# Attention scores from stacked key halves in two fp32r passes, and the third block attended whole ahead of the last slab's second half

## The chip, the cores and the metric

The kernel runs on one core of a Trainium2 chip. The metric is the time of one execution in microseconds of device time; the times below are medians over runs on the chip. A profiled execution gives the trace that the views are taken from: its own time is a little larger than its span, which goes from the first to the last recorded instruction.

## The reference

A trunk of two layers over 512 tokens of width 1024, all in float32. Each layer has a mixer and a PEER stage (16384 experts, product-key routing). The part that the change touches is the first of the mixer's three branches, differential attention with 4 heads, two 64-wide maps per head and blocks of 128 queries:

```python
def block(args):
    qi, bi = args
    s = jnp.einsum('bqhmd,bkhmd->bhmqk', qi, k).astype(jnp.float32) * scale
    qpos = bi * Q_BLOCK + jnp.arange(Q_BLOCK)
    mask = kpos[None, :] <= qpos[:, None]
    p = jax.nn.softmax(jnp.where(mask, s, -jnp.inf), axis=-1)
    a = p[:, :, 0] - lam * p[:, :, 1]
    return jnp.einsum('bhqk,bkhe->bqhe', a.astype(v.dtype), v)
```

The other two branches are a gated short convolution over 256 channels and gated linear attention (GLA). The three outputs are concatenated and multiplied by `w_out`, and the result is added to the residual `x`.

## The kernel before

**How products are made.** Nearly all large products run in float32r, a form of float32 that TensorE takes in one pass with fewer bits. Each operand is kept as a high half (the value rounded to float32r) and a low half (what the rounding left). `split` (L83) makes them: ScalarE copies the value into the high half, VectorE subtracts that from the value into the low half. `mm3` (L77) then adds three products: high by high (L79), high by low (L80), low by high (L81). The small products (scores, transposes, the product with the values) run in plain float32: one such matmul of the program shows as two TensorE instructions in the trace, each with its own weight load.

**The mixer** (L221). The input projection is done in column slabs of 256: `across` (L268) gives channels on the partitions and 512 tokens along the row, `down` (L277) gives tokens on the partitions. Each slab loads its weights in four pieces, splits them, and runs 48 or 96 matmuls. The order is: gate and value slabs, GLA's queries and keys, attention's queries and keys (tiles `qT` and `kT`, 128 partitions = 2 maps x 64 dims, 4 heads, 512 tokens), rotary turning of both (`rope`, L463, which writes its results back by DMAs from GpSimd's queue, L471), attention's values (tile `va`), and the convolution's three slabs 2048, 1792 and 1536 (L378, L381, L393). GLA's steps are strewn between the slabs (`fill`).

**Attention.** There are four query blocks of 128. Block `tb` sees (tb+1)*128 keys, so its score products are 128, 256, 384 and 512 wide. For each block `turned_queries` (L473) copies the two maps of the queries into a tile `qz` whose other 64 partitions are zero (cleared once per layer at L369), so that a contraction over all 128 partitions of `kT` counts one map alone. `head_weights` (L479) makes for one head and each of its two maps, called a score half below, one plain float32 product (L486) and one bfloat16 product with the causal mask (L487) into the same PSUM tile; then come the maximum, the exponentials and the difference of the two maps (L488 to L498). `diff_attention` (L502) transposes the weights (L512) and multiplies them by the values (L516). Blocks 0 and 1 are attended around the convolution's slabs (L375, L380), two heads of block 2 between the two halves of the last slab (L395), the rest of block 2 and block 3 inside the output projection's loop (L434).

**The output projection.** When the slabs' pools close, a pool `wout` opens (L400) with `woraw`, `mh`, `ml`, `woh` and `wol`. Its eight pieces of weights are loaded and split; `out_proj` (L420) takes the token blocks in turn, its last operands being the attention outputs `mh` and `ml`.

**The next stage.** `peer` (L709) opens a pool `ustream` whose tiles are `uraw` (3 x 4 KB per partition), `uwa` (2 x 8 KB), `uwb` (2 x 8 KB) and `ht`, in the order of first use. It loads and splits the first three pieces of the query weights (L778 to L783; the splits show as L729 and L730), and runs their products over the first 256 tokens (L787) while the last token block of the mixer is being normed.

**What sets the order.** The framework schedules the instructions at compile time: an instruction goes where its inputs are ready on the engine, and among those that are ready the order of the program decides. On the chip each engine then works off its list in that order. Memory is handed out as a stack: a pool that opens after another was closed gets the same addresses, and its tiles wait, each for itself, for the last use of what lay there. On the left side the mixer's pool `mix` comes first (`dgain`, `cw`, `qT`, `kT`, `va` and small ones), then the slabs' pools; `wout` opens where the slabs' pools began, and `ustream` where `mix` began.

## Time and profile before

| | |
|---|---|
| median of 3 runs | 2962.35 us (2961.81 to 2962.88) |
| the profiled execution: time | 2958.37 us |
| the profiled execution: span | 2956.6 us |
| TensorE busy | 2925.6 us, 99% of the span |
| VectorE busy | 2394.7 us, 81% |
| ScalarE busy | 1256.3 us, 42% |
| GpSimd busy | 716.0 us, 24% |
| mean granted TensorE clock | 0.999 |

The two mixers lie at about 0 to 269 us and, with its first products made at the end of the first PEER stage, from about 1480 to 1737 us. A line of the timeline gives start, duration, engine, source line, operation, output and inputs, shapes and a count of merged instructions; what stands in brackets is idle time of the engine ahead of it and what ended it. TensorE's matmuls are pipelined, so the duration of one is longer than the step from its start to the next start; it is the step that counts for the time. "PEld" is the weight load, which can run beneath the matmul ahead of it.

### The profile page before, as it was taken

The page shows a single profiled execution, that of the slowest core. Times are in us where ns is not written, and L with a number is a line of the kernel's source. Part 1 is how long each engine was busy: PE and PEld are TensorE (multiplying, and loading weights), DVE is VectorE, ACT ScalarE, POOL GpSimd, SP SyncE. Part 2 cuts the span into 40 slices and gives each one's busy share as a digit, 9 for nine tenths or more (in the row PEclk, how much of TensorE's full clock was granted, in tenths as well). Part 3 has the DMA queues.
Part 4 walks back from the last instruction along what each step waited for, and adds up shares of the span by engine and source line. Part 5 has one row for each costly group of instructions (what it writes and reads, how often), then busy time and mean ns, then how long its engine had stood idle before and what let it go on. Part 6 is the DMA issues. An engine that isn't in the chain of part 4 may idle for free.

```text
span 2956.6 us, 44538 instructions
## 1 busy us (share of the span) xinstructions
PE 2925.6 (99%) x16262; PEld 2606.0 (88%) x16262; DVE 2394.7 (81%) x4754; ACT 1256.3 (42%) x1860; POOL 716.0 (24%) x617
## 2 busy tenths in 40 slices
PE   8999999999999999999999999999999999999998
PEld 7878899999999999888888788999999999988887
DVE  6676999976887788877866769999768787888778
ACT  6253355665333332333453433556653333333333
POOL 1200000222444455222012000012225444452220
PEclk9999999999999999999999999999999999999999
DMA  4322257999999998999633222679999999989995
GB/s 130 92 72 77 93 172 250 321 301 362 348 338 326 330 346 310 368 333 342 251 96 90 67 82 86 205 253 330 303 351 356 333 337 332 332 316 358 346 347 203
DMA packets 335835, 760.24 MB, mean 257 GB/s; under 512 B 30688, under 2 KB 191360, under 8 KB 331520
## 3 DMA queue, kind: packets, MB, share of 16 engines
q1 hardware_dynamic: 160624, 435.19, 41.4%
q0 software_dynamic: 75776, 271.62, 26.0%
q10 hardware_dynamic: 99216, 50.60, 5.7%
q8 instruction: 127, 2.08, 0.3%
q14 instruction: 92, 0.75, 0.1%
HBM read 673.15 MB, written 81.00 MB: 255 GB/s over the span
## 4 chain that ended last, share of the span: by engine, by line
PE 84%; DVE 11%; ACT 2%; issue 2%; DMA 1%; SPq 0%; DVEq 0%; ACTq 0%
PE pv L80 11%; PE pv L81 11%; PE pv L79 11%; PE psh L79 9%; PE psh L81 9%; PE psh L80 9%; PE psp L80 2%; PE psp L81 2%; PE psp L79 2%; PE psq L80 2%; PE psq L79 2%; PE psq L81 2%; PE pss L486 1%; PE psg L1211 1%; PE pss L764 1%
## 5 line engine op out<-in xcount | busy, mean ns | idle before, releaser
L827 POOL DMA_INDIRECT row<-in_u_rows,idx x256 | 349.1, 1363 | 1337.6 <-DVE row L834 627.8
L80 PE MATMUL pv<-vl,wh 128*128 128x512 f32 x1500 | 583.9, 389 | 0.4 <-DVE vl L931 0.3
L81 PE MATMUL pv<-vh,wl 128*128 128x512 f32 x1500 | 583.4, 389 | 0.0
L79 PE MATMUL pv<-vh,wh 128*128 128x512 f32 x1500 | 583.2, 389 | 0.0
L827 POOL DMA_INDIRECT row<-in_v_rows,idx x256 | 315.7, 1233 | 597.0 <-DVE yacc L843 548.2
L745 ACT ACTIVATE ht<-psh 128x384 f32<-128x384 f32 x256 | 125.7, 491 | 742.1 <-PE psh L81 741.9
L931 DVE TENSOR_TENSOR vl<-vraw,vh 128x1024 fp32r<-128x1024 f32 x250 | 305.9, 1224 | 115.2 <-ACT vh L936 104.2
L79 PE MATMUL psh<-ahi,uwb 128*128 128x384 f32 x1024 | 346.9, 339 | 0.0
L79 PE MATMUL psh<-ahi,uwa 128*128 128x384 f32 x1024 | 346.4, 338 | 0.0
L81 PE MATMUL psh<-ahi,uwa 128*128 128x384 f32 x1024 | 344.6, 337 | 0.7 <-DVE uwa L730 0.7
L80 PE MATMUL psh<-alo,uwa 128*128 128x384 f32 x1024 | 344.3, 336 | 0.0
L80 PE MATMUL psh<-alo,uwb 128*128 128x384 f32 x1024 | 344.2, 336 | 0.0
L81 PE MATMUL psh<-ahi,uwb 128*128 128x384 f32 x1024 | 344.1, 336 | 0.0
L81 PEld LDWEIGHTS pv<-vh,wl 128*128 128x128 f32 x1500 | 281.4, 188 | 59.6 <-DVE wl L931 1.0
L80 PEld LDWEIGHTS pv<-vl,wh 128*128 128x128 f32 x1500 | 281.4, 188 | 56.6 <-DVE vl L931 2.2
L79 PEld LDWEIGHTS pv<-vh,wh 128*128 128x128 f32 x1500 | 281.6, 188 | 53.9
L843 DVE SCALAR_TENSOR_TENSOR yacc<-row,wk,yacc 128x1024 f32<-128x1024 f32 x254 | 325.2, 1280 | 1.7
L944 ACT CAST wh<-ht 128x384 fp32r<-128x384 f32 x250 | 127.9, 512 | 433.6 <-DVE ht L1096 417.0
L834 DVE SCALAR_TENSOR_TENSOR row<-row,xg 128x1024 f32<-128x1024 f32 x256 | 308.0, 1219 | 0.0
L730 DVE TENSOR_TENSOR uwa<-uraw,uwa 128x1024 fp32r<-128x1024 f32 x144 | 175.7, 1223 | 134.7 <-ACT uwa L729 134.5
L936 ACT CAST vh<-vraw 128x1024 fp32r<-128x1024 f32 x250 | 262.6, 1050 | 9.7 <-DMA vraw<-in_v_rows 9.7
L730 DVE TENSOR_TENSOR uwb<-uraw,uwb 128x1024 fp32r<-128x1024 f32 x144 | 175.8, 1222 | 105.9 <-ACT uwb L729 105.9
(361 smaller groups left out, 5708.6 us busy)
## 6 DMA issues: line engine op xcount, KB each, us to landing
uraw<-in_peer_u SPq DMA_DIRECT2D x256, 512.0 KB, 5.6
vraw<-in_v_rows SPq DMA_DIRECT2D x256, 512.0 KB, 6.5
G<-stg ACTq DMA_DIRECT2D x48, 1024.0 KB, 7.6
g<-G SPq DMA_DIRECT2D x32, 1536.0 KB, 10.0
H<-ht SPq DMA_DIRECT2D x144, 192.0 KB, 4.7
ht<-H SPq DMA_DIRECT2D x144, 192.0 KB, 6.5
wraw<-in_w_in SPq DMA_DIRECT2D x84, 256.0 KB, 3.2
uraw<-in_peer_w_q SPq DMA_DIRECT2D x32, 512.0 KB, 3.5
```

What stands on the lines that cost most here:

```text
L79: mm(ps, ah, bh, start=first, stop=False)
L80: mm(ps, ah, bl, start=False, stop=False)
L81: mm(ps, al, bh, start=False, stop=last)
L486: nc.tensor.matmul(ps[:, 0:nk], qz[:, h, m], kT[:, h, 0:nk], start=True, stop=False)
L730: self.last = pin(nc.vector.tensor_tensor(lo, src, hi.bitcast(F32), op=OP.subtract))
L745: pin(nc.scalar.activation(hs[c], ps, AF.Gelu))
L827: nc.gpsimd.indirect_dma_start(out=r, out_offset=None, in_=ins[name], in_offset=bass.IndirectOffsetOnAxis(ap=idx[:, k:k + 1], axis=0))
L834: nc.vector.scalar_tensor_tensor(r, r, 1.0, xg, op0=OP.mult, op1=OP.mult, accum_out=hd[:, k:k + 1])
L843: nc.vector.scalar_tensor_tensor(yacc, r, wk[:, k:k + 1], yacc, op0=OP.mult, op1=OP.add)
L931: self.last = pin(nc.vector.tensor_tensor(lo, src, hi.bitcast(F32), op=OP.subtract))
L936: pin(nc.scalar.copy(vh[c], vs[c]))
L944: pin(nc.scalar.copy(wh[c], hs[c]))
```

## The change

The queries and keys are split into high and low halves as float32r. For each map m the tile `ks[m]` holds, on the 64 partitions of that map, the high halves of its keys, and on the other 64 partitions the low halves of the same keys, brought there by a DMA from GpSimd's queue. `qa` holds the high halves of the queries on both halves of the partitions (again by a DMA), `qb` the low halves. One pass over 128 partitions gives high by high plus high by low; a second pass over the 64 partitions of the map gives low by high. `qz`, its clearing and `turned_queries` go.

The order changes with it: the first two blocks' keys and queries are split and stacked ahead of slab 2048, block 0 is attended behind that slab, then the other keys and block 2's queries are stacked, block 1 is attended behind slab 1792, and the whole of block 2 between the two halves of slab 1536. Block 3 stays in the output projection's loop. `qT` and `kT` move out of `mix` into a pool `rawqk` of their own, which opens behind `mix` and closes with the slabs' pools.

```diff
             cw = mp.tile([P, 2, 3], F32, name="cw")
-            qT = mp.tile([P, 4, T], F32, name="qT")
-            kT = mp.tile([P, 4, T], F32, name="kT")
             va = mp.tile([P, TB, T], F32, name="va")
+            wc = mc.enter_context(ExitStack())
+            raw_qk = wc.enter_context(tc.tile_pool(name="rawqk", bufs=1, reuse_waits="tile"))
+            qT = raw_qk.tile([P, 4, T], F32, name="qT")
+            kT = raw_qk.tile([P, 4, T], F32, name="kT")
...
-            with ExitStack() as wc:
+            with wc:
...
-                qz = [ap.tile([P, 4, 2, P], F32, name=f"qz{i}", bufs=1) for i in range(2)]
-                for t in qz:
-                    nc.gpsimd.memset(t, 0.0)
+                ks = [ap.tile([P, 4, T], F32R, name=f"ks{i}", bufs=1) for i in range(2)]
+                kl = wc.enter_context(tc.tile_pool(name="klow", bufs=2, side="right", reuse_waits="tile"))
+                half = [slice(64 * m, 64 * m + 64) for m in range(2)]
+
+                def stack_keys(tb):
+                    t = slice(tb * P, tb * P + P)
+                    lo = kl.tile([P, 4, P], F32R, tag="klo", name="klo")
+                    for m in range(2):
+                        r = half[m]
+                        self.split(ks[m][r, :, t], lo[r], kT[r, :, t])
+                        nc.gpsimd.dma_start(ks[m][half[1 - m], :, t], lo[r])
+
+                def stack_queries(tb):
+                    qa = ap.tile([P, 2, 4, P], F32R, tag="qa", name="qa")
+                    qb = ap.tile([P, 4, P], F32R, tag="qb", name="qb")
+                    for m in range(2):
+                        r = half[m]
+                        self.split(qa[r, m], qb[r], qT[r, :, tb * P:tb * P + P])
+                        nc.gpsimd.dma_start(qa[half[1 - m], m], qa[r, m])
+                    return qa, qb
...
-                attend(0)
+                stack_keys(0)
+                qs[0] = stack_queries(0)
+                stack_keys(1)
+                qs[1] = stack_queries(1)
                 z = qp.tile([P, 2, T + 2], F32, tag="z", name="z", bufs=1)
                 nc.vector.memset(z[:, :, 0:2], 0.0)
                 for j, ps in across(2048):
                     nc.scalar.copy(z[:, j, 2:], ps)
-                attend(1)
+                attend(0)
+                for tb in (2, 3):
+                    stack_keys(tb)
+                qs[2] = stack_queries(2)
                 for j, ps in across(1792):
                     nc.vector.tensor_tensor(z[:, j, 2:], ps, z[:, j, 2:], op=OP.mult)
+                attend(1)
+                qs[3] = stack_queries(3)
...
                 for j, ps in across(1536):
                     if j == 0:
-                        self.turned_queries(2, qT, qz[0])
-                        early = [self.head_weights(2, h, kT, qz[0], lam, ap) for h in range(2)]
+                        attend(2)
                     nc.vector.tensor_tensor(ys[j], ys[j], ps, op=OP.mult)
...
                 for tb in range(TB):
-                    if tb > 1:
-                        attend(tb, early if tb == 2 else ())
+                    if tb > 2:
+                        attend(tb)
...
         for m in range(2):
             ps = self.psA.tile([P, T], F32, tag="a", name="pss")
-            nc.tensor.matmul(ps[:, 0:nk], qz[:, h, m], kT[:, h, 0:nk], start=True, stop=False)
+            r = slice(64 * m, 64 * m + 64)
+            nc.tensor.matmul(ps[:, 0:nk], qs[0][:, m, h], ks[m][:, h, 0:nk], start=True, stop=False)
+            nc.tensor.matmul(ps[:, 0:nk], qs[1][r, h], ks[m][r, h, 0:nk], start=False, stop=False)
             nc.tensor.matmul(ps[:, tb * P:nk], self.identb, self.causal, start=False, stop=True)
```

19 lines of the change are left out of this document (6 added, 13 removed).

## The prediction

> **What bounds the kernel now.** I read the page first: the busy shares, then the chain that ended last.
>
> ```profile
> PE 2925.6 (99%) x16262; PEld 2606.0 (88%) x16262; DVE 2394.7 (81%) x4754; ACT 1256.3 (42%) x1860; POOL 716.0 (24%) x617
> PE 84%; DVE 11%; ACT 2%; issue 2%; DMA 1%; SPq 0%; DVEq 0%; ACTq 0%
> ```
>
> TensorE is busy nearly throughout and carries 84% of the chain; VectorE carries most of the rest. So a microsecond of score products removed counts in full, unless VectorE becomes late. The shares are averages, so next come the first layer's stretches in which the change works: 147 to 196.5 us (blocks 0 and 1, the convolution's slabs), 196.5 to 226 (blocks 2 and 3, the first output products), 226 to 268.8 (the other output products).
>
> ```profile
> core 0: us, PE busy (x) PEld busy (x) DVE busy (x) ACT busy (x) POOL busy (x), PEclk, DMA share, GB/s
> 147.00:196.50 49.50, 49.36 (x244) 37.55 (x243) 35.85 (x112) 24.78 (x72) 0.00 (x0) 1.00 0.16 49
> 196.50:226.00 29.50, 28.77 (x139) 19.02 (x138) 26.79 (x58) 18.87 (x37) 0.00 (x0) 1.00 0.32 107
> 226.00:268.80 42.80, 42.43 (x217) 34.32 (x216) 24.58 (x59) 13.32 (x26) 0.00 (x0) 1.00 0.19 63
> ```
>
> In the 79 us of the first two rows TensorE idles 0.14 + 0.73 = 0.87 us. VectorE is at 72% in the first and at 91% in the second (26.79 of 29.50), and only there does TensorE lose much, 2.5% of the stretch. ScalarE is at 55%, GpSimd does nothing there, and the clock is 1.00. All sums below are per layer, and taken twice.
>
> **The score products now.** A score half is one plain product (two instructions) and the mask. By the count, each width has 32 instructions in two layers, which is 8 halves per layer. The steps come from the timeline, start to next start.
>
> ```profile
> L486 PE MATMUL pss<-kT,qz x128: 272/482/653, 150.8 to 1682.2; 128*128 128x128 f32 x32, 128*128 128x256 f32 x32, 128*128 128x384 f32 x32, 128*128 128x512 f32 x32
> ```
>
> ```profile
> 151.33 0.38 PE L486 MATMUL pss<-kT,qz 128*128 128x128 f32 x2
> 151.55 0.22 PE L487 MATMUL pss<-causal,identb 128*128 128x128 bf16 x1
> 151.61 0.44 PE L486 MATMUL pss<-kT,qz 128*128 128x128 f32 x2
> 151.88 0.22 PE L487 MATMUL pss<-causal,identb 128*128 128x128 bf16 x1
> 151.94 0.33 PE L486 MATMUL pss<-kT,qz 128*128 128x128 f32 x1
> ...
> 164.08 0.65 PE L486 MATMUL pss<-kT,qz 128*128 128x256 f32 x2
> 164.62 0.43 PE L486 MATMUL pss<-kT,qz 128*128 128x256 f32 x1
> ...
> 188.64 0.86 PE L486 MATMUL pss<-kT,qz 128*128 128x384 f32 x2
> 189.39 0.54 PE L486 MATMUL pss<-kT,qz 128*128 128x384 f32 x1
> ...
> 207.46 1.08 PE L486 MATMUL pss<-kT,qz 128*128 128x512 f32 x2
> 208.41 0.48 PE L80 MATMUL pso<-wol,mgh 128*128 128x512 f32 x1
> ```
>
> A half takes 151.94 - 151.61 = 0.33 us at width 128, of which the mask is 0.06; and 0.54, 0.75 and 0.95 at widths 256, 384 and 512, mask included. Together 2.57 us, times 8 is 20.6 us per layer. Behind a mask the pair takes 0.27, otherwise 0.22 (151.55 - 151.33), so 0.05 of weight load shows behind the short mask.
>
> **The score products after.** A half becomes two fp32r passes and the mask. The price of one pass is the step of the kernel's other fp32r products:
>
> ```profile
> 1552.74 0.39 PE L80 MATMUL psp<-alo,wh 128*128 128x512 f32 x1
> 1552.97 0.40 PE L81 MATMUL psp<-ahi,wl 128*128 128x512 f32 x1
> ...
> 702.09 0.34 PE L81 MATMUL psh<-ahi,uwb 128*128 128x384 f32 x1
> 702.26 0.34 PE L79 MATMUL psh<-ahi,uwb 128*128 128x384 f32 x1
> ...
> 136.58 0.28 PE L81 MATMUL psp<-wh,alo 128*128 128x256 f32 x1
> 136.69 0.28 PE L79 MATMUL psp<-wh,ahi 128*128 128x256 f32 x1
> ```
>
> That is 0.23, 0.17 and 0.11 for 512, 384 and 256 columns. For 128 no row exists: between 0.06 (half of 256) and 0.11 (no gain below 256); I take 0.06, since the steps fall in proportion. Two passes at all four widths cost 2 x 0.57 = 1.14 us.
>
> But the second pass contracts over 64 rows, and the products before and behind it over 128. The only 64-row products of this kernel with 128-row ones beside them are GLA's (L648):
>
> ```profile
> 1553.29 0.30 PEld L648 LDWEIGHTS psu<-gv,kdT 64*128 64x128 f32 x4 [0.36 <-issue]
> 1553.29 0.49 PE L648 MATMUL psu<-gv,kdT 64*128 64x256 f32 x2
> 1553.61 0.38 PE L648 MATMUL psu<-gv,kdT 64*128 64x256 f32 x2
> 1553.92 0.73 PEld L610 LDWEIGHTS pst<-qs,ks 128*128 128x128 f32 x4 [0.33 <-issue]
> 1553.92 0.48 PE L610 MATMUL pst<-qs,ks 128*128 128x256 f32 x1
> ```
>
> The pass begun at 1552.97 is through 0.23 later, at 1553.20; the 64-row pair begins at 1553.29: 0.09 lost. Its first step is 1553.61 - 1553.29 = 0.32 against 0.22 for the next pair by the same geometry, so 0.10 of weight load is exposed: the load did not slip beneath the product ahead, and its idle time says "issue", that is, nothing the profile shows. On the way back, 1553.61 + 0.22 = 1553.83 against 1553.92: again 0.09. A switch costs about 0.09 + 0.10 = 0.19. [...]
>
> Each half has two switches: in, 0.19, and out to the mask, where I take 0.09 and half of the exposed load, 0.14, since the mask's bfloat16 identity is a smaller load than those rows'. With 0.06 for the mask and 0.05 for the load behind it, a half is 2s + 0.44, with s the step of its width. Over four widths: 1.14 + 1.76 = 2.90 against 2.57, times 8 is +2.6 us per layer. Bounds: no price for switches (2s + 0.11) gives 1.58, or -7.9 us; 0.19 both ways and 0.11 at width 128 give 3.20, or +5.0. I take the middle value because it goes by the one row with the same geometry.
>
> **The splits, copies and new waits.** Sixteen splits and sixteen DMAs per layer come in; eight copies to `qz` on ScalarE and the clearing on GpSimd go.
>
> ```profile
> 148.95 1.89 DVE L85 TENSOR_TENSOR wl<-wraw,wh 128x512 fp32r<-128x512 f32 x3
> 132.18 1.56 POOL L471 DMA_DIRECT2D kT<-rot  x3 [11.56 <-DVE rot L468]
> kT<-rot POOLq DMA_DIRECT2D x8, 64.0 KB, 3.2
> ```
>
> A subtraction of 512 elements takes 1.89 / 3 = 0.63 us, and I give one over 64 partitions with rows of the same length the same, so VectorE gets 16 x 0.62 = 9.9 us. GpSimd spends 0.52 us on an issue, 8.3 us in a stretch where it does nothing: free. The copies land some 3 us after issue; blocks 0 and 1 have slab 2048 (some 11 us of products) between stacking and use, blocks 2 and 3 a slab each: free, and without that cover a landing each. ScalarE's eight more copies have room. A score product that did wait for a landing would hold the slab's products behind it on TensorE, hence the rival below.
>
> VectorE then has 35.85 + 26.79 + 9.9 = 72.5 us in 79 + 2.6 = 81.6, 89%, and evenly, since block 2 moved forward out of the crowded row. By that row's rate (2.5%) TensorE loses 2.0 us instead of 0.87: +1.1, between -0.9 (all gone) and +2.1. Block 2's whole attention only trades places with output products; it issues no DMA and passes only the slab's weight loads, whose buffers TensorE frees as before.
>
> **The hand-over to the next stage.** Moving `qT` and `kT` out of `mix` shifts the addresses of `wout`, and so what `ustream` lies on.
>
> ```profile
> 239.28 0.75 DVE L537 SCALAR_TENSOR_TENSOR ml<-htr,dgain,mh 128x512 fp32r<-128x512 f32 x1 [0.88 <-ACT mh L536]
> 240.06 1.41 SPq L726 DMA_DIRECT2D uraw<-in_peer_w_q  x3
> 263.26 2.01 ACT L729 CAST uwa<-uraw 128x1024 fp32r<-128x1024 f32 x2
> 268.57 0.39 PE L81 MATMUL pso<-woh,ml 128*128 128x512 f32 x1
> 268.77 2.00 ACT L729 CAST uwb<-uraw 128x1024 fp32r<-128x1024 f32 x2 [3.49 <-PE pso L80]
> 268.80 0.28 PE L79 MATMUL psq<-ahi,uwa 128*128 128x256 f32 x1
> 269.85 1.23 DVE L730 TENSOR_TENSOR uwb<-uraw,uwb 128x1024 fp32r<-128x1024 f32 x1 [2.78 <-ACT uwb L729]
> ```
>
> By the tiles' sizes `mix` has about 25.0 KB per partition (three tiles of 8 KB and small ones), then `woraw` to 33.2, `mh` to 41.4, `ml` behind. `ustream` begins at 0: `uraw` to 12.3, `uwa` to 28.7, `uwb` to 45.1. The rows agree: `uraw` is loaded as soon as `dgain`'s last reader ends (240.03), `uwa` is split early, and `uwb` waits until 268.77 for `mh`'s last reader, L80. So TensorE goes on without a gap, at 268.80. After, `mix` ends at about 8.6 KB, `woraw` at 16.8, `mh` at 25.0, `ml` at 33.2: `uwa` itself lies on `mh` and `ml`. Its first cast moves to 268.77, its subtraction to where `uwb`'s is now, 269.85 to 271.08. Behind the waiting cast on ScalarE stand only the other casts; TensorE has nothing else ready, and can begin with two products of 0.11 that need the high half alone. Idle: 271.08 - 268.80 - 0.23 = 2.05 us per layer (0 if the addresses fall otherwise, 2.3 without the two products).
>
> **The sum.** Per layer 2.6 + 2.05 + 1.1 = 5.75, in two layers +11.5. The profiled execution took 2958.37 us (span 2956.6, 1.8 around it), so 2969.9 there; it lies 3.98 below the median, 2962.35, which I keep: 2973.9, say 2974.
>
> **The rivals.** First, the other side: the 64-row pass streams like any other. For it: the "issue" gaps are few rows of plain float32 with two loads per product, which an fp32r pass has not. Against it: they recur at each change and in both directions. Then the scores give -7.9 us, but VectorE's 72.5 us become the bound of a stretch that would be 71: I take 75, 4.0 less than 79, and with the hand-over's +2.05 it is -1.95 per layer: 2958.4, between 2953.4 (VectorE without a gap: 2 x (72.5 - 79 + 2.05) = -8.9) and 2966.4 (it gives all of the gain back, and only 2 x 2.05 is left). It decides below (7.9 - 2.05 - 1.1) / 32 = 0.15 us for both switches of a half together, where I have 0.33.
>
> Second, the hand-over stays hidden: `uwa` does not fall on `mh`. For it: the addresses are worked out, not shown. Against it: `uraw`'s start, `uwa`'s early cast and `uwb`'s wait all fit them. Then 2 x (2.6 + 1.1) = +7.4: 2969.7.
>
> Third, the copies are late: sixteen issues in one GpSimd queue, two for each stack, and the splits ahead of them on a fuller VectorE. One landing of 3.2 us and an issue, about 4 us, shown once per layer, gives +8: 2982. Against it: a slab lies between.
>
> **How the numbers follow.** A measurement of this kernel can tell 0.2%, 5.9 us, from no change: faster is below 2956.4, slower above 2968.3. My forecast has 0.45 (slower 0.43, same 0.02; its own range by the bounds 2971 to 2981). The first rival has 0.38 (faster 0.21 when VectorE packs well, same 0.15, slower 0.02), the second 0.10 (half slower, half same, since 7.4 is barely past the mark), the third 0.07, slower. Faster 0.21, same 0.22, slower 0.57. The range runs from the first rival's middle part, 2955, to the forecast's upper bound, 2981, and leaves out some 0.15.
>
> **What would show it.** Right: L486's successors for the second pass show the 64-row shape with idle "issue" of some 0.3 us on PEld at every half; a half at width 512 takes 0.90, at 128 0.56; the first cast into `uwa` starts only after the last `pso` product, and TensorE idles about 2 us there. Wrong: a half at width 128 of 0.25 or less (the first rival); casts into `uwa` some 5 us ahead of the last `pso` product (the second); score products with DMA from GpSimd's queue as their releaser (the third); VectorE above 95% with TensorE idle by several per cent between the slabs.

## The result, and the profile after

The changed kernel takes 2993.6 us (median of 4 runs, 2993.27 to 2997.88), the kernel before 2962.08 us in the same comparison. The ratio is 1.0114, with a 95% interval of 1.0098 to 1.0130: slower by 31.5 us. The forecast had the direction, but only 11.5 us, and a range that ended at 2981.

The same views as before, now of the changed kernel. First the busy shares and the chain that ended last.

```profile
PE 2946.2 (98%) x16262; PEld 2614.9 (87%) x16262; DVE 2410.0 (81%) x4786; ACT 1266.8 (42%) x1876; POOL 732.0 (24%) x645
PE 81%; DVE 11%; DMA 3%; ACT 2%; issue 2%; SPq 0%; ACTq 0%; DVEq 0%
```

TensorE is busy for 20.6 us more with the same number of instructions, and its share of the chain has gone down. DMA has risen from 1% to 3% of the chain: somewhere a transfer is now waited for.

The stretches come next. To compare them, they go from one mark to the next, from the last transposes of GLA to the first product of the next stage, in both layers. First the kernel before, then the changed one. The column behind POOL is the granted clock.

```profile
146.22:268.80 122.58, 121.34 (x603) 91.67 (x602) 87.22 (x229) 57.55 (x134) 0.00 (x0) 1.00 0.20 68
...
1613.87:1736.81 122.94, 120.97 (x602) 91.77 (x601) 87.11 (x229) 57.67 (x134) 0.00 (x0) 1.00 0.21 67
```

```profile
145.40:283.55 138.15, 130.46 (x603) 95.55 (x601) 93.06 (x244) 62.02 (x141) 9.13 (x16) 0.94 0.28 71
...
1630.94:1769.31 138.37, 129.33 (x603) 94.81 (x601) 93.08 (x244) 62.04 (x141) 9.15 (x16) 0.95 0.27 71
```

The stretch of the attention and the output projection is 15.6 us longer in the first layer and 15.4 us in the second. In the first layer TensorE's idle time goes from 1.24 to 7.69 us, and the granted clock, which was 1.00, falls to 0.94: 0.06 x 138.15 is 8.3 us. These two are about 14.7 of the 15.6 us.

The same can be added up over the whole span. Idle time is the span less TensorE's busy time. Clock lost is half of all the time at 0.50 (the record of the granted clock has no other value below 1.00), up to TensorE's last product: what the clock does in the last microseconds, where TensorE has nothing left to do, costs nothing. Work is the busy time, with the time at 0.50 counted half. Idle time at 0.50 stands in both of the first columns, so the three add up to a little more than the span (0.8 us for the changed kernel, 3.1 at most in the runs below).

| profiled run | span | clock lost | idle | work |
|---|---|---|---|---|
| before | 2956.6 | 0.0 | 31.0 | 2925.6 |
| after | 2991.6 | 17.1 | 45.4 | 2929.9 |
| difference | +35.0 | +17.1 | +14.4 | +4.3 |

So about an eighth of the loss is work. Nearly half is a lowered clock, which the prediction does not contain. The list of waits on TensorE in the first layer names the idle times, with the sum, the count and the longest:

```profile
PE pss L509 <- ACT e L517: 2.8, 1, 2.8
PE pso L80 <- DVE wol L85: 2.2, 2, 1.7
PE psq L79 <- ACT uwa L750: 0.9, 1, 0.9
...
PE psq L81 <- DVE uwa L751: 0.8, 1, 0.8
```

There are three holes: at block 0's scores, at the first output products, and at the hand-over. The second layer has the same three. In both layers together the first has 6.6 us of idle time (2.82 and 3.82) and 8.5 us of lost clock behind it, the second 3.4 and 6.8, the hand-over 3.3 and 1.7; with the 4.3 us of work this is nearly all of the loss. The timeline shows who waits for whom at the first:

```profile
156.33 1.41 DVE L85 TENSOR_TENSOR klo<-kT,ks 64x512 fp32r<-64x512 f32 x2 [0.69 <-DMA ks<-klo]
157.77 0.69 DVE L85 TENSOR_TENSOR wl<-wraw,wh 128x512 fp32r<-128x512 f32 x1
158.38 1.39 DVE L85 TENSOR_TENSOR klo<-kT,ks 64x512 fp32r<-64x512 f32 x2
158.49 2.92 SPq L265 DMA_DIRECT2D wraw<-in_w_in  x2
159.80 0.49 DVE L512 TENSOR_REDUCE st<-pss 128x1 f32<-128x128 f32 x2
...
162.50 0.62 ACT L84 CAST wh<-wraw 128x512 fp32r<-128x512 f32 x1 [3.25 <-DMA wraw<-in_w_in]
163.03 0.36 ACT L517 ACTIVATE e<-pss,st 128x128 f32<-128x128 f32 x1
163.53 0.48 PE L509 MATMUL pss<-ks,qa 128*128 128x128 f32 x1 [2.82 <-ACT e L517]
```

Read it backwards. TensorE waits for the exponentials because four score tiles fill the PSUM buffers. ScalarE could make them, but stands at a cast of slab 1792's last weight piece, 3.25 us, until its load lands. That load was issued only at 158.49, when VectorE had freed a buffer with the subtraction begun at 157.77. VectorE was late because the key splits of blocks 2 and 3 stand in its list, and one of them had waited for a copy to release `klo`. The maxima at 159.80 are behind the same splits. No score product waits for a landing itself.

Behind this hole the clock falls. Five stretches of 1 us:

```profile
161.00:162.00 1.00, 0.00 (x0) 0.00 (x0) 1.00 (x6) 0.00 (x0) 0.00 (x0) 1.00 1.46 271
162.00:163.00 1.00, 0.00 (x0) 0.00 (x0) 0.16 (x2) 0.50 (x1) 0.00 (x0) 0.67 1.23 215
164.00:165.00 1.00, 1.00 (x5) 0.77 (x4) 0.36 (x4) 1.00 (x5) 0.00 (x0) 0.50 0.00 0
172.00:173.00 1.00, 1.00 (x4) 0.77 (x4) 0.56 (x2) 0.00 (x0) 0.00 (x0) 0.71 0.38 68
173.00:174.00 1.00, 1.00 (x6) 0.49 (x5) 0.00 (x0) 0.27 (x1) 0.00 (x0) 1.00 0.00 0
```

The granted clock is 0.50 from 162.33 to 172.57 us: the means 0.67 and 0.71 of the second and fourth stretch give these two ends. Half of the 10.24 us, 5.12, is lost, more than the hole itself. Of this, 4.5 us fall on TensorE's work, from 163.53 on.

### The profile page after: what moved, and what is told of

Its sections match the earlier page's. It is cut to its first block, busy times and chain, and to the rows that moved or that the text cites. A ratio compares the mean times of both kernels' runs of the same rounds, so it can differ in the third digit from the quotient of the medians.

```text
span 2991.6 us, 44666 instructions
## 1 busy us (share of the span) xinstructions
PE 2946.2 (98%) x16262; PEld 2614.9 (87%) x16262; DVE 2410.0 (81%) x4786; ACT 1266.8 (42%) x1876; POOL 732.0 (24%) x645
## 4 chain that ended last, share of the span: by engine, by line
PE 81%; DVE 11%; DMA 3%; ACT 2%; issue 2%; SPq 0%; ACTq 0%; DVEq 0%
PE pv L80 11%; PE pv L81 11%; PE pv L79 11%; PE psh L79 9%; PE psh L81 9%; PE psh L80 9%; PE psp L81 2%; PE psp L80 2%; PE psp L79 2%; PE psq L81 2%; PE psq L79 2%; PE psq L80 2%; PE pss L785 1%; PE psg L1232 1%; DVE uwa L751 1%
```

## The experiments

All ratios are to the kernel before in the same comparison. The last three columns are worked out as in the table above, from the one profiled run of each, which need not be the median one. In e1_nocopy, e2_full, e10_hand, e13_fill and b7_spread_pool, 1.7 us of the lost clock lie in a PEER stage, away from the edits.

| run | median us | ratio (95%) | clock lost | idle | work |
|---|---|---|---|---|---|
| e1_nocopy | 2990.0 | 1.0098 (1.0081 to 1.0114) | 11.9 | 44.7 | 2931.6 |
| e2_full | 2974.2 | 1.0045 (1.0029 to 1.0061) | 11.9 | 47.8 | 2914.6 |
| e6_late | 2989.7 | 1.0101 (1.0084 to 1.0118) | 13.7 | 41.4 | 2931.6 |
| e10_hand | 2983.2 | 1.0073 (1.0056 to 1.0090) | 11.9 | 41.4 | 2931.0 |
| e11_pin | 2995.8 | 1.0114 (1.0097 to 1.0131) | 13.7 | 45.3 | 2928.8 |
| e4_block2 | 2988.2 | 1.0090 (1.0074 to 1.0107) | 13.7 | 42.1 | 2929.6 |
| e5_order_alone | 2966.8 | 1.0020 (1.0010 to 1.0030) | 0.0 | 32.5 | 2927.9 |
| e13_fill | 2997.4 | 1.0120 (1.0103 to 1.0137) | 17.1 | 49.6 | 2935.7 |
| e15_narrow64 | 2999.8 | 1.0139 (1.0122 to 1.0156) | 17.1 | 32.9 | 2946.5 |
| e16_narrow128 | 2973.1 | 1.0047 (1.0031 to 1.0064) | 0.0 | 33.9 | 2935.6 |
| b3_full_pin_hand | 2973.0 | 1.0043 (1.0028 to 1.0058) | 13.7 | 42.8 | 2914.4 |
| b4_spread | 2968.3 | 1.0026 (1.0016 to 1.0036) | 1.7 | 41.7 | 2916.8 |
| b5_onecopy | 2973.0 | 1.0042 (1.0025 to 1.0059) | 8.5 | 45.2 | 2914.0 |
| b6_spread_ord | 2973.3 | 1.0038 (1.0023 to 1.0052) | 11.9 | 47.6 | 2913.4 |
| b7_spread_pool | 2977.4 | 1.0055 (1.0038 to 1.0072) | 6.8 | 50.5 | 2918.5 |
| b9_mixed | 2973.6 | 1.0046 (1.0032 to 1.0059) | 6.8 | 50.4 | 2916.7 |
| b10_mixed_whole | 2988.4 | 1.0096 (1.0080 to 1.0111) | 10.2 | 58.3 | 2921.0 |
| b11_mixed_early | 2968.1 | 1.0016 (1.0007 to 1.0025) | 5.1 | 44.1 | 2918.1 |

**Is it the switch of rows?** One line changes: the second pass runs over all 128 partitions. The other 64 partitions of `qb` hold the other map's low query halves and meet low key halves of this map. So the added term does not belong to the score, and is small: low times low.

```diff
-            nc.tensor.matmul(ps[:, 0:nk], qs[1][r, h], ks[m][r, h, 0:nk], start=False, stop=False)
+            nc.tensor.matmul(ps[:, 0:nk], qs[1][:, h], ks[m][:, h, 0:nk], start=False, stop=False)
```

> The changed kernel with one edit: the second pass contracts over all 128 partitions (low queries of both maps against the stacked keys; the added term is low times low). No 64-row product is left in the scores. Theory of the prediction, a price per switch of 128 to 64 rows and back: a score half falls from 0.53 to about 0.25 us at width 128 and from 0.88 to about 0.57 at 512, 32 halves times 0.3 = 9.6 us less TensorE work per layer. If TensorE sets the time, 2993.6 - 19 = 2974; if the halves get shorter but the waits for VectorE and ScalarE take the place, 2985 to 2993. Rival, no price of a switch: halves as before, 2993.

Measured: 2974.2 us, 19.4 below the changed kernel, as the price per switch said. The timeline of a half of width 128, first in the changed kernel (first pass, second pass, mask, next half), then in this one:

```profile
157.72 0.30 PE L509 MATMUL pss<-ks,qa 128*128 128x128 f32 x1
157.95 0.32 PE L510 MATMUL pss<-ks,qb 64*128 64x128 f32 x1
158.21 0.23 PE L511 MATMUL pss<-causal,identb 128*128 128x128 bf16 x1
158.25 0.31 PE L509 MATMUL pss<-ks,qa 128*128 128x128 f32 x1
```

```profile
157.10 0.31 PE L509 MATMUL pss<-ks,qa 128*128 128x128 f32 x1
157.24 0.27 PE L510 MATMUL pss<-ks,qb 128*128 128x128 f32 x1
157.36 0.23 PE L511 MATMUL pss<-causal,identb 128*128 128x128 bf16 x1
157.39 0.30 PE L509 MATMUL pss<-ks,qa 128*128 128x128 f32 x1
```

The half falls from 0.53 to 0.29 us; by the same reading it falls from 0.60 to 0.32, 0.72 to 0.43 and 0.88 to 0.59 us at widths 256, 384 and 512. That is 0.24 to 0.29 us for the two switches of a half. Work falls by 15.3 us over two layers, 0.24 us for each of the 64 halves. Idle time did not fall with it, and the clock still falls behind the holes, 10.2 us in the two mixers for 17.1: the holes have another cause.

**The first hole: traffic or queue?** Two runs. One leaves the copies out (GpSimd writes zeros there), the other writes the later stacking behind slab 1792, so that one weight piece of the slab is split ahead of the key splits.

```diff
-                        nc.gpsimd.dma_start(ks[m][half[1 - m], :, t], lo[r])
+                        nc.gpsimd.memset(ks[m][half[1 - m], :, t].bitcast(F32), 0.0)
...
-                        nc.gpsimd.dma_start(qa[half[1 - m], m], qa[r, m])
+                        nc.gpsimd.memset(qa[half[1 - m], m].bitcast(F32), 0.0)
```

> The changed kernel (2993.6 us) without its 16 copies per layer from partition half to partition half; GpSimd writes zeros into those halves instead, so the product of high queries and low keys is left out. The splits, the passes and the order stay. Theory one, the copies' traffic: they fill the DMA engines from 151 to 160 us, the last weight piece of slab 1792 lands late, ScalarE stands at its cast (3.25 us at 162.50) with the exponentials behind it, TensorE idles 2.82 us and then runs at a granted clock of 0.50 for some 10 us; without the copies this hole is gone in both layers: 2.82 + 5.1 us each, about 2978. Rival, the queue: the piece is late because its load waits for a buffer that VectorE frees only behind the eight key splits; then the hole stays and the time is 2990 or more.

```diff
-                for tb in (2, 3):
-                    stack_keys(tb)
-                qs[2] = stack_queries(2)
                 for j, ps in across(1792):
                     nc.vector.tensor_tensor(z[:, j, 2:], ps, z[:, j, 2:], op=OP.mult)
+                for tb in (2, 3):
+                    stack_keys(tb)
+                qs[2] = stack_queries(2)
                 attend(1)
```

> The changed kernel with the stacking of the keys of blocks 2 and 3 written behind slab 1792 in place of ahead of it: on ScalarE and VectorE one weight piece of the slab is now split ahead of the four key casts. The queue theory: that piece's buffer comes free some 3 us earlier, the last piece's load is issued at about 155.5 in place of 158.49 us and lands before ScalarE needs it, the idle 2.82 us and the slow clock behind it go: about 2978. The traffic theory: the load is earlier but shares the DMA engines with the copies, a part of the wait stays, 2983 to 2992.

Measured: 2990.0 and 2989.7 us. In both runs the hole shrinks, in the first layer from 2.82 to 1.1 us, in the second from 3.82 to 1.07 and 0.81, and neither takes it away. So neither cause is the whole one, and the 2978 us that each theory gave for its cause alone did not come. The rival of the first run had the time, 2990 or more, but expected the hole to stay as it was. What ScalarE waits for in front of block 0's exponentials is different in the two, first without the copies, then with the weight piece ahead:

```profile
161.68 0.37 ACT L517 ACTIVATE e<-pss,st 128x128 f32<-128x128 f32 x1 [1.76 <-DVE st L514]
```

```profile
160.89 0.62 ACT L84 CAST wh<-wraw 128x512 fp32r<-128x512 f32 x1 [1.05 <-DMA wraw<-in_w_in]
```

Without the copies what is left is the queue: the maxima, which stand behind the splits on VectorE. With the weight piece ahead what is left is the traffic: the last piece's load is issued 1.5 us earlier, at 156.97, but its cast still starts only 3.9 us behind the issue, where it was 4.0, and 3.2 without the copies. That is what the traffic theory of that run said, 2983 to 2992. And the clock falls all the same. In the run with the later keys, 1.09 us of idle time (first row) is followed by 3.41 us of lost clock:

```profile
160.00:162.00 2.00, 0.91 (x5) 0.43 (x4) 1.97 (x7) 1.11 (x4) 0.76 (x2) 1.00 1.25 168
162.00:164.00 2.00, 2.00 (x11) 1.42 (x11) 1.78 (x9) 1.02 (x6) 0.00 (x0) 0.87 0.79 174
...
168.00:170.00 2.00, 2.00 (x8) 1.61 (x7) 1.25 (x6) 1.07 (x5) 0.21 (x1) 0.50 0.35 66
170.00:172.00 2.00, 2.00 (x11) 1.37 (x9) 0.49 (x2) 0.27 (x1) 0.00 (x0) 0.93 0.00 0
```

Next, the key splits of blocks 2 and 3, and these alone, are moved behind block 1 and kept there (`keep_in_program_order` puts an instruction behind all that its engine was given before).

```diff
+                            pin = tc.keep_in_program_order
+                            pin(nc.scalar.copy(ks[m][r, :, t], kT[r, :, t]))
+                            pin(nc.vector.tensor_tensor(lo[r], kT[r, :, t], ks[m][r, :, t].bitcast(F32), op=OP.subtract))
...
                 attend(1)
+                for tb in (2, 3):
+                    stack_keys(tb)
+                qs[2] = stack_queries(2)
```

> The changed kernel with the stacking of the keys of blocks 2 and 3 behind block 1's attention, and its splits pinned there, so that they cannot stand ahead of block 0's maxima on VectorE nor ahead of its exponentials on ScalarE. Copies, passes and everything else as in the changed kernel. The runs before left 1.07 us of the hole at block 0 without the copies and 1.09 us with one weight piece put ahead; in both the key splits still stood before the maxima. Queue theory: now the hole goes wholly, the granted clock stays at 1.00 there, and the stretch from the last GLA transposes to the next stage's first product, 138.15 us in the changed kernel, falls by 2.82 + 5.1 to about 130; in all about 2978. Rival: the hole moves to block 2, whose keys are now stacked just ahead of their use, and the time stays above 2988.

Measured: 2995.8 us. The first hole is gone (0.26 us), and the rival came about: block 2's first score product now waits for the copy of its keys. The wait on TensorE there:

```profile
PE pss L514 <- DMA ks<-klo: 3.9, 1, 3.9
```

With it goes the longest loss of clock behind any wait in these runs, 6.83 us in each layer. So the hole stands where the stacking stands, and a copy does have a landing to wait for once a slab no longer covers it.

**The hand-over.** The high halves of the output weights become eight tiles in the order of their use, ahead of `mh` and `ml`.

```diff
-                mh = op_.tile([P, 4, T], F32R, name="mh")
-                ml = op_.tile([P, 4, T], F32R, name="ml")
-                wh = op_.tile([P, KD, D], F32R, name="woh")
+                wh = {k: op_.tile([P, D], F32R, name=f"woh{k}") for k in korder}
+                mh = op_.tile([P, 4, T], F32R, name="mh")
+                ml = op_.tile([P, 4, T], F32R, name="ml")
```

> The changed kernel with the high halves of the output weights in eight tiles, one per 128 rows, in the order of use, placed ahead of the attention outputs mh and ml. The tiles of the next stage's first splits then lie on weights whose last use is some 4 us ahead of the last output product. Theory: TensorE's idle time at the hand-over (0.91 + 0.76 us) and the slow clock behind it (1.7 us) go in both layers: 3.4 x 2 = 6.7 less, about 2987. Rival: the idle time there has another cause (the norm of the last token block), then 2993.

Measured: 2983.2 us, 10.4 below the changed kernel. The timeline of the changed kernel, and then of this one, at the last output product and the first ones of the next stage:

```profile
282.25 0.39 PE L81 MATMUL pso<-woh,ml 128*128 128x512 f32 x1
282.45 1.99 ACT L750 CAST uwa<-uraw 128x1024 fp32r<-128x1024 f32 x2 [5.40 <-PE pso L80]
283.52 2.36 DVE L751 TENSOR_TENSOR uwa<-uraw,uwa 128x1024 fp32r<-128x1024 f32 x2 [5.05 <-ACT uwa L750]
283.55 0.38 PE L79 MATMUL psq<-ahi,uwa 128*128 128x256 f32 x1 [0.91 <-ACT uwa L750]
284.81 0.39 PE L81 MATMUL psq<-ahi,uwa 128*128 128x256 f32 x1 [0.76 <-DVE uwa L751]
```

```profile
281.00 0.39 PE L81 MATMUL pso<-woh,ml 128*128 128x512 f32 x1
281.23 0.28 PE L79 MATMUL psq<-ahi,uwa 128*128 128x256 f32 x1
```

The idle time of 0.91 + 0.76 us is gone, in both layers. That is 3.3 us, and the clock lost there in the first layer was 1.7: together some 5 of the 10.4. Most of the rest lies at the first hole, whose lost clock is 3.41 and 1.71 us in this run against 5.12 and 3.41, and whose idle time is 1.3 us less in both layers together. The edit does not touch that place, so this part is probably not its own; no run shows it.

**The order, and block 2.** In the first run of these, block 2 goes back to where it was; in the second, the kernel before gets the order of the change and nothing else.

```diff
                     if j == 0:
-                        attend(2)
+                        early = [self.head_weights(2, h, ks, qs[2], lam, ap) for h in range(2)]
...
-                    if tb > 2:
-                        attend(tb)
+                    if tb > 1:
+                        attend(tb, early if tb == 2 else ())
```

> The changed kernel with block 2 as in the kernel before: the weights of two heads between the halves of slab 1536, the rest in the output projection's loop. Scores, splits, copies and the stacking order stay. Theory: the second hole (0.62 us at the values' product and 1.71 us at the first product with the low halves of the output weights, then about 3.4 us for the clock) comes from block 2's eight exponentials and four copies ahead of the casts of the output weights on ScalarE; with half of block 2 behind them it goes: 5.7 us per layer, about 2982. Rival: it comes from block 3's slower scores and maxima, then 2991 to 2996.

```diff
-                attend(0)
                 z = qp.tile([P, 2, T + 2], F32, tag="z", name="z", bufs=1)
...
-                attend(1)
+                attend(0)
...
+                attend(1)
...
-                        self.turned_queries(2, qT, qz[0])
-                        early = [self.head_weights(2, h, kT, qz[0], lam, ap) for h in range(2)]
+                        attend(2)
```

> The kernel before with the order of the change alone: block 0 behind slab 2048, block 1 behind slab 1792, the whole of block 2 between the halves of slab 1536. Scores stay plain float32 from the padded queries, no splits, no copies, no move of tiles. Theory, the holes need the new splits and the 64-row passes: 2955 to 2968, as before. Rival, the order alone makes the second hole: 2 x 5.7 us more, about 2973.

Measured: 2988.2 and 2966.8 us. With block 2 back, the second hole only changes its shape: TensorE waits 1.24 us for the casts of the output weights at 232.6, which costs no clock, and 5.12 us of clock are lost in the first layer behind two waits of 0.66 and 0.62 us at 206.4 and 207.6, between block 2's products. Half of what was expected came. The order alone costs 0.2% (0.1 to 0.3), as the theory said. Its profile (of the fastest of its ten runs, 2962.1 us) has a hole of 1.44 us in each layer and no loss of clock at all:

```profile
206.00:208.00 2.00, 1.46 (x8) 0.70 (x7) 2.00 (x7) 0.56 (x1) 0.00 (x0) 1.00 0.03 8
208.00:210.00 2.00, 1.09 (x4) 0.53 (x5) 1.84 (x9) 2.00 (x5) 0.00 (x0) 1.00 0.00 0
```

So 1.44 us beside plain float32 scores cost no clock, and 1.09 us beside the new ones cost 3.41 us. The length of a wait alone does not decide.

**What lowers the clock?** Three runs. The first puts a wide throwaway product in front of each half of block 0.

```diff
+            if tb == 0:
+                nc.tensor.matmul(ps, self.fill[:, 0, 0:P], self.fill[:, 0], start=True, stop=True)
             nc.tensor.matmul(ps[:, 0:nk], qs[0][:, m, h], ks[m][:, h, 0:nk], start=True, stop=False)
```

> The changed kernel with one throwaway fp32r product of 512 columns (0.23 us) in front of each of block 0's eight score halves, into the same PSUM tile, overwritten by the real one: 1.84 us more TensorE work per layer. In the runs before, the granted clock fell to 0.50 for one to four times 3.41 us (1.71 us lost each) behind idle times of 0.8 to 4.0 us next to the bursts of narrow score passes, while 1.44 us of idle time beside plain float32 scores cost none. Activity theory: the clock goes by how much the array works in a stretch of about 3.4 us, and the narrow passes with their waits count as little; with the array working more in the burst, the loss behind block 0 (5.12 and 3.42 us) falls by at least 1.71 in each layer and the time does not rise: 2980 to 2993. Idle theory: only the idle time in front counts; it stays at about 2 to 3 us, the loss stays, and the time rises by up to 3.7: 2993 to 2997.

The other two put a burst of narrow products into the kernel before. The first has 64-row products in turn with 128-row ones; the second has the whole tile (`0:P`) in place of `0:64`.

```diff
+            if tb == h == m == 0:
+                a = self.fill
+                for i in range(24):
+                    k, c = i % 8, i // 8 * P
+                    self.tc.keep_in_program_order(nc.tensor.matmul(ps[:, 0:P], a[:, k, c:c + P], a[:, k, 0:P], start=True, stop=True))
+                    self.tc.keep_in_program_order(nc.tensor.matmul(ps[:, 0:P], a[0:64, k, c:c + P], a[0:64, k, 0:P], start=True, stop=True))
```

> The kernel before with 48 throwaway fp32r products of 128 columns per layer in front of block 0's scores, alternately over 128 and over 64 partitions, overwritten by the real ones: a burst like that of the changed kernel's scores, some 0.25 us each, 12 us per layer, in which TensorE is never idle. Activity theory: the granted clock goes by the work in the array, and such a burst counts as little; the clock falls to 0.50 inside or behind it with no idle time in front, and the time is 24 us and some 7 to 20 more: 2990 to 3010. Idle theory: without idle time the clock stays at 1.00 and the time is 2962 + 24 = 2986 or a little less.

> As the run before, but all 48 throwaway products contract over 128 partitions, so that there is no switch of rows. Price-per-switch theory: a product takes 0.1 to 0.15 us in place of 0.25, so the burst is 5 to 7 us per layer. Activity theory: the clock falls less than in the burst with 64 rows or not at all. Idle theory: clock 1.00, 2962 + 12 = 2974.

Measured: 2997.4, 2999.8 and 2973.1 us. The filler did not help: the losses behind block 0 are 5.12 us in both layers, and the idle time in front is still 2.71 and 1.77 us; what the activity theory said of this run did not come, and the time lies at the upper end of the idle theory's. The two bursts came out at the times that the activity theory gave for the first and both theories for the second. With 64-row products, TensorE is never idle (2.00 of 2.00), and still the clock falls 3 us into the burst:

```profile
146.00:148.00 2.00, 2.00 (x15) 1.65 (x13) 0.70 (x2) 1.91 (x4) 0.00 (x0) 1.00 0.00 0
148.00:150.00 2.00, 2.00 (x9) 1.51 (x8) 2.00 (x5) 1.98 (x5) 0.00 (x0) 0.92 0.00 0
150.00:152.00 2.00, 2.00 (x6) 1.42 (x5) 0.51 (x1) 1.76 (x3) 0.00 (x0) 0.50 0.74 214
...
170.00:172.00 2.00, 2.00 (x13) 1.52 (x12) 1.73 (x10) 1.47 (x3) 0.00 (x0) 0.96 0.00 0
```

With 128 rows throughout, the same number of products, one behind the other, leaves it at 1.00 (the middle stretch of the burst):

```profile
...
148.00:150.00 2.00, 2.00 (x21) 2.00 (x19) 2.00 (x4) 1.98 (x5) 0.00 (x0) 1.00 0.02 4
...
```

A pair of products takes 0.51 us in the first and 0.22 in the second, so the two switches of a pair cost 0.29 us, and in two layers the burst with them loses 17.1 us of clock, the burst without none. Whether the clock goes by the rows in use or by the gaps of the switch, these two do not tell apart.

**Versions that keep the good part.** Eight runs combine the 128-partition second pass with repairs. The first two differ in where the later keys are stacked, the third copies all keys of a map in one DMA, the fourth and fifth change block 2's place and the engine of the subtractions, and the last three leave blocks 0 and 1 in plain float32.

> Three edits together on the changed kernel: the second pass over 128 partitions, the pinned later stacking of the keys of blocks 2 and 3, and the output weights' high halves in tiles of their own ahead of mh and ml. If their gains add (19.4 and 10.4 measured alone, some 16 expected of the pinning): 2993.6 - 46 = 2948, below the kernel before. If the first hole only moves: about 2962.

Its edits are those of e2_full, e11_pin and e10_hand. The next keeps the pins, but stacks one block at a time (the diff is against the changed kernel):

```diff
                 attend(0)
-                for tb in (2, 3):
-                    stack_keys(tb)
+                stack_keys(2)
                 qs[2] = stack_queries(2)
...
                 attend(1)
+                stack_keys(3)
                 qs[3] = stack_queries(3)
```

> The changed kernel with four edits: the second pass over 128 partitions; the output weights' high halves in tiles of their own ahead of mh and ml; block 2's keys and queries stacked and pinned behind block 0's attention, and block 3's keys behind block 1's. Theory: the first hole falls below 1 us since only blocks 0 and 1 are stacked ahead of it, block 2's wait for its copies (3.9 us where all four were stacked behind block 1) goes since a slab lies between, and TensorE's work is 14 us below that of the kernel before: 2950 to 2960. Rival: the weight pieces still come late behind the copies of blocks 0 and 1 and the clock still falls twice per layer: 2965 to 2973.

```diff
-                        self.split(ks[m][r, :, t], lo[r], kT[r, :, t])
-                        nc.gpsimd.dma_start(ks[m][half[1 - m], :, t], lo[r])
+                        self.split(ks[m][r], lo[r], kT[r])
+                        nc.gpsimd.dma_start(ks[m][half[1 - m]], lo[r])
```

> As the run before (128-partition second pass, output weights ahead of mh and ml), but all the keys of a map are split in one instruction per engine and copied in one DMA with rows of 8 KB in place of four with rows of 512 bytes: 2 key copies per layer in place of 8, ahead of slab 2048's end. Theory of the traffic: long rows take the DMA engines for a shorter time, the weight pieces land in some 3 us, the hole at block 0 falls below 1 us: 2950 to 2960. Rival, VectorE: the key splits (about 5 us) now all stand ahead of block 0's maxima and block 0's scores wait for the copies: a hole of 2 to 4 us with a slow clock in each layer, 2960 to 2975.

Measured: 2973.0, 2968.3 and 2973.0 us. In the first the gains do not add: the hole moves to block 2's keys as in e11_pin, 3.9 us in both layers, and 2.2 us of the first hole stay in the first layer; the time is above the rival's 2962 too. Spreading the stacks, one behind block 0 and one behind block 1, gives the time of its rival, not of its theory; it leaves 1.7 us of lost clock in its profile and no wait above 1.3 us; its TensorE work is 8.8 us below that of the kernel before, and its idle time 10.7 us above. (That profile is of a run of 2962.0 us, the fastest of its nine.) The one long copy has the rival's hole, 3.87 us at block 0.

The next is b4_spread with the edit of e4_block2; the one after it is b4_spread with the subtractions moved:

> The version with the 128-partition second pass, the output weights ahead of mh and ml and the spread stacking (2968.3 us, where the profile has 4.3 us of clock lost and 41.5 us of idle time against 2.2 and 30.4 in the kernel before), and block 2 again as before: two heads between the slab's halves, the rest in the output loop. Theory: the idle time between 199 and 229 us (some 5.5 us per layer) comes from block 2's softmax crowding the casts of the output weights, and half of it goes: 2958 to 2964. Rival: it comes from VectorE's load, which the splits raise wherever block 2 stands: 2966 to 2972.

```diff
-                            pin(nc.vector.tensor_tensor(lo[r], kT[r, :, t], ks[m][r, :, t].bitcast(F32), op=OP.subtract))
+                            pin(nc.gpsimd.tensor_tensor(lo[r], kT[r, :, t], ks[m][r, :, t].bitcast(F32), op=OP.subtract))
```

> The same version (2968.3 us), block 2 whole between the halves, with the 16 subtractions of the key and query splits per layer on GpSimd in place of VectorE. Theory: VectorE has 9.9 us less per layer, and the idle time in front of TensorE in the stretch falls by several us: 2952 to 2962. Rival: GpSimd's subtraction is slower and holds the copies behind it in its queue, so that scores wait for them: 2968 or more.

Measured: 2973.3 and 2977.4 us, both the rival. With block 2 divided, the idle time rises from 41.7 to 47.6 us; with the subtractions on GpSimd it rises to 50.5 us, so taking this work off VectorE bought nothing here; whether GpSimd's slower subtractions (1.3 to 1.5 us for 0.7) hide a gain was not taken apart.

In the last three, blocks 0 and 1 keep their padded queries and the order of the kernel before, and the key splits follow one by one:

```diff
+                def plain(tb):
+                    for m in range(2):
+                        nc.scalar.copy(qz[tb][half[m], :, m], qT[half[m], :, tb * P:tb * P + P])
+                    qs[tb] = (qz[tb], kT)
...
+            if tb < 2:
+                nc.tensor.matmul(ps[:, 0:nk], qs[0][:, h, m], qs[1][:, h, 0:nk], start=True, stop=False)
```

> Blocks 0 and 1 keep the plain float32 scores of the kernel before, in its order (block 0 ahead of slab 2048, block 1 behind it), since a half of width 128 costs 0.29 us with two full passes against 0.33; blocks 2 and 3 take stacked keys and two passes over 128 partitions. The key splits are pinned one block at a time behind blocks 0 and 1 and the slabs; two heads of block 2 between the halves of slab 1536, the rest in the output loop; output weights ahead of mh and ml. Work theory: a half of width 384 and 512 saves about 0.3 and 0.38 us, 5.4 us per layer or 11 in all; with nothing narrow or late at block 0 the first hole and its clock go: 2950 to 2958, below the kernel before. Rival: the splits on VectorE and ScalarE around block 2 give it back: 2960 to 2970.

```diff
-                        early = [self.head_weights(2, h, ks, qs[2], lam, ap) for h in range(2)]
+                        attend(2)
                         stack_keys(3)
                         qs[3] = stack_queries(3)
```

> As the run before, but the whole of block 2 between the halves of slab 1536. Earlier runs with the 128-partition pass: whole 2968.3, split 2973.3. Work theory: 2950 to 2958. Rival: 2960 to 2970; if the exponentials of the whole block again crowd the casts of the output weights, it is slower than the run before.

The last goes back to b9_mixed and moves the stacking:

```diff
                 stack_keys(0)
-                attend(1)
                 stack_keys(1)
+                attend(1)
+                stack_keys(2)
...
-                stack_keys(2)
+                stack_keys(3)
                 qs[2] = stack_queries(2)
+                qs[3] = stack_queries(3)
...
-                        stack_keys(3)
-                        qs[3] = stack_queries(3)
```

> As the mixed version with two heads of block 2 between the halves (2973.6 us; 5.2 us of idle time per layer before a transpose whose PSUM tile waits for VectorE, where the key splits of block 3 stand ahead, and 3.4 us of lost clock behind it), but every key split comes one step earlier: blocks 0 and 1 behind slab 2048, block 2 behind block 1, block 3 and its queries behind slab 1792. Theory: VectorE reaches the reading of that PSUM tile some 2.8 us earlier or more, half or more of the 5.8 us of idle time goes and the clock with it: 2955 to 2963. Rival: the splits only displace other work in front of TensorE: 2968 or more.

Measured: 2973.6, 2988.4 and 2968.1 us. The first two lie above what theory and rival gave, and the second is slower than the first, as its rival said it could be. The first hole is gone with its cause, as expected, and idle time comes back at block 2. In the first of the three TensorE stands there for 5.2 us, until VectorE has read a PSUM tile behind the key splits; one step earlier, in the last, that wait is down to 1.9 us, as the theory said, but the time is at the lower end of the rival's, 2968 or more. None of the eight beats the kernel before: the best has a ratio of 1.0016 (1.0007 to 1.0025).

## Why the prediction was wrong

**The steps that held.** The score products: a half takes 0.53 us at width 128 and 0.88 at 512 (from the row at 210.03 to the one at 210.91), where 0.56 and 0.90 were worked out, and the work of TensorE rose by 4.3 us over both layers where 5.2 were expected.

```profile
210.03 0.48 PE L509 MATMUL pss<-ks,qa 128*128 128x512 f32 x1
210.44 0.49 PE L510 MATMUL pss<-ks,qb 64*128 64x512 f32 x1
210.87 0.23 PE L511 MATMUL pss<-causal,identb 128*128 128x128 bf16 x1
210.91 0.48 PE L509 MATMUL pss<-ks,qa 128*128 128x512 f32 x1
```

At the small widths this closeness is partly luck, for two errors nearly cancel: an fp32r pass of 128 columns takes 0.11 us (0.22 for a pair in e16_narrow128), the upper bound, not 0.06, and two switches cost 0.24 to 0.29 us (the halves of e2_full, the bursts), where 0.33 stood. The first rival needed less than 0.15 and is out. The hand-over: its mechanism, its place and its first row were right, and idle time was 1.67 us per layer for 2.05; so the second rival is out too.

**The step that failed: the edits costed at nothing.** "The copies land some 3 us after issue ... free", and the splits only as a load on VectorE. Two things were left out. The splits of blocks 2 and 3, which no one needs before block 2, have their inputs ready early, so they were scheduled ahead of block 0's maxima and of the weight piece that slab 1792 needs; what waits is not their reader but what stands behind them. And the copies are under way while that weight piece is: the time of the packets of GpSimd's queue from 151 to 163 us is 89.7% of that of the 16 DMA engines, and the piece's cast starts 4.0 us behind the issue of its load, against 3.2 without the copies. In the sum it is the term of the stalls, +1.1 per layer, which went by VectorE's mean rate: up to the next stage's first product the idle time rose by 6.45 and 7.07 us in the two layers, of which only 0.91 each is the hand-over's. Idle time rose by 14.4 us in all, where hand-over and stalls together were put at (2.05 + 1.1) x 2 = 6.3. Since leaving out either the traffic or a part of the place in the queue left 1.1 of the first hole's 2.82 us, both carry it. The third rival was nearest, 2982, but its wait, a score product that waits for a landing, is in the changed kernel not there; it appeared only where the stacking stands closer to its reader (e11_pin, b3_full_pin_hand, b10_mixed_whole).

**The term that was missing: the clock.** The sum went by a granted clock of 1.00 throughout. It fell to 0.50 at five of the six holes (all but the hand-over in the second layer), 17.1 us in all, more than the idle time rose. It also fell without any idle time, in the burst with 64-row passes between 128-row ones (17.1 us lost), and not in the one with 128 rows throughout (0.0). The holes do it without such passes too: e2_full has none in its scores and loses 10.2 us in its mixers. e5_order_alone shows a hole that does not.

**Which hole lowers the clock.** No run was made for this, but the traces show it in part. The clock changes on a grid of 3.41 us: in the first mixer of the changed kernel at 162.33, 172.57, 220.36, 227.19, 285.21 and 288.62 us, which are 3, 14, 2, 17 and 1 steps of 3.413 us apart. Those in its second mixer, at 1650.54, 1657.37, 1705.16 and 1711.98 us, are 399, 2, 14 and 2 such steps further on, and in twelve of the other runs the changes that stretches of 2 us show lie on a grid of the same step, to within 0.03 us. The hand-over shows what that does. Its two idle times, 0.91 and 0.76 us, are the same in both layers; here are the steps of the grid in which they lie, in the first layer with the step behind them, then in the second:

```profile
281.80:285.21 3.41, 1.74 (x9) 1.08 (x8) 1.69 (x2) 2.76 (x3) 0.00 (x0) 1.00 0.00 0
285.21:288.62 3.41, 3.41 (x18) 3.41 (x18) 2.41 (x3) 0.60 (x2) 0.00 (x0) 0.50 0.76 217
...
1766.60:1770.01 3.41, 2.30 (x10) 1.43 (x8) 0.72 (x1) 1.80 (x2) 0.00 (x0) 1.00 0.00 0
1770.01:1773.42 3.41, 2.85 (x24) 2.85 (x25) 3.37 (x4) 1.14 (x2) 0.00 (x0) 1.00 0.51 150
```

In the first layer both fall into one step, TensorE is idle for 1.67 of 3.41 us, and the next step runs at 0.50. In the second a line of the grid divides them into 1.11 and 0.56 us, and the clock stays. So the same two waits cost clock in the layer in which they fell into one step, and none in the other. From TensorE's first product to its last, five steps at full clock in the changed kernel are followed by half clock: TensorE is idle in them for 1.62, 1.71, 1.67, 2.94 and 1.28 us (from 158.92, 216.95, 281.80, 1647.13 and 1701.74 us). In each of its other steps at full clock it is idle for 1.11 us or less. In b6_spread_ord one step of the first PEER stage has 1.28 us too (from 757.6 us), and the clock stays at 1.00. In e6_late, among 64-row score products, 1.0 to 1.1 us of idle time in a step went ahead of half clock in the first layer, 0.81 us or less in the second, and in the bursts of e15_narrow64 none.

**What stays open.** Why the burst with 64-row products loses 17.1 us of clock and the one without them none, and why 1.28 us of idle time in a step went ahead of half clock at one place and not at another, is not settled. The second hole, 3.4 us of idle time and 6.8 of clock, has no cause shown: the order alone does not make it, and with block 2 back it only changes its shape. And why the idle time around block 2 returns in every version, wherever the splits stand, was not taken apart further than to the queues named above.

## What to carry to other kernels

A wait on TensorE had two prices here: its own length, and the half clock behind it, which was as much again and more (14.4 us more idle time, 17.1 us of clock). In the changed kernel, waits that together left TensorE idle for 1.62 us or more of a step of 3.41 us paid both, and so did those that left 1.28 us. The two switches between products over 128 and over 64 partitions cost 0.24 to 0.29 us per score half. They can be avoided where the other half can be filled with something harmless: here the other map's low halves did it in one line, and the kernel became 19 us faster. And work that is ready early is not free because its reader comes late: look at what stands behind it on its engine, and which loads are under way with its copies.

## What was not expected of the hardware

The lost clock came in portions: 1.71, 3.41, 5.12 and 6.83 us in the runs' holes, one to four times 1.71, which is half of 3.41 us, one step of the grid, at a granted clock of 0.50. Its length did not follow the idle time alone: at the hand-over in the first layer 1.67 us of idle time in a step went ahead of one step of half clock, and in e15_narrow64 TensorE has no idle time and the clock is 0.50 for some 20.5 us (about 149.7 to 170.2), six times 3.41.
